# Joining the second half of a dilated-attention layer's tokens: softmax weights carried through DRAM, or built on chip and spread by TensorE

## Chip, cores and metric

One core of one Trainium2 chip. The metric is the device time of one execution in microseconds (us); the kernel before stands at 2389.81 us, the median of three runs. "Change" below means the edited kernel; a row or a page named without more belongs to the kernel before.

## What is computed

Two encoder layers over T = 1024 tokens of D = 1024 features, each a token mixer and a SwiGLU FFN with a pre-RMSNorm and a gated residual. The second layer's mixer is dilated attention in three head groups; only its join is touched:

```
for gi, (window, dil) in enumerate(((128, 1), (512, 4), (2048, 16))):
    o, lse = banded_attention(to_strided(q[:, :, gi], dil), ...)   # 8 query heads, 2 KV heads, 64 wide
    outs.append(from_strided(o, b, dil)); lses.append(from_strided(lse, b, dil))
alpha = softmax(stack(lses), axis=0)          # weight of each group, per position and head
o = einsum('nbshg,nbshgd->bshgd', alpha, stack(outs))
return o.reshape(b, s, 512) @ w_out
x = x + g1 * y;  h = rmsnorm(x, norm_ffn) * (1 + sc2) + sh2
x = x + g2 * ((silu(gate) * up) @ ffn_w_out)
```

## The kernel before

Activations lie with features on the partitions, D as eight k-tiles of 128 rows, the tokens as two halves t = 0 and 1 of HT = 512 columns. Each fp32 product of a weight and an activation is three matmuls on split operands (`acc3`, L297): high by high (L300), high by low (L301), low by high (L302). A weight tile arrives by a DMA (`load_w`, L182), is rounded by ScalarE (L179) and its low part is subtracted by GpSimd (L180).

Layer 2 (`layer_b`, L907) runs 48 units of attention. A unit's first half (`probs`, L495) is scores on TensorE (L506, L507), bias and minimum on VectorE (L509) and exponentials on ScalarE (L514). Its second half (`weigh`, L517) transposes the probabilities (L534), splits them into high and low part (ScalarE L536, VectorE L537), multiplies by the values (L528) and writes the output (ScalarE L549, VectorE L550). Between the units TensorE is fed from a list of fill work in a fixed order, with a table of due points (`fill_start`, FILL_B): projections, then the out-projection of the first token half (`out_0`; residual L370, squares L217 and L218), that half's norm (`norm_half`; sums L222, statistics on GpSimd, broadcast L260, then L272, L273, L275, L276, L278 per k-tile) and, last, 48 matmuls of the FFN's first feature block on that half (`up_early`).

Groups 1 and 2 hold their tokens in strided order, and their outputs go to DRAM (od[1], od[2]) and come back. The softmax statistics take this way: `stat_out` (L1052) transposes minimum and sum of a group and half (copy L1062, TensorE L1063, ScalarE L1070) and stores them (sd, DMAs L1068, L1072, L1075). `alphas(t)` (L1077) loads the three groups' statistics (ml_all, L1082), permutes them into token order (VectorE copies L1086 to L1088), forms the weights in small operations on 64 partitions (L1090 to L1100, exponential L1094) and stores them (ad, L1101). `combine_load` (L1121) loads two groups' outputs (al<-od, L1114, L1115) and the weights, each row repeated over 64 partitions (al<-ad, L1128). `combine` (L1131) forms, per 128 rows g of 0 to 3, o2 and o3 times their weights (L1141, L1143), o1 times its weight (L1145, on GpSimd for t = 1), two sums (L1146, L1147), and the high and low part for the out-projection (ScalarE L1148, VectorE L1149).

The first half is joined at units 33 to 37. The second half is joined after the last unit: `stat_out(0, 1)`, `alphas(1)`, `combine_load(1, 0)`, the last units' second halves, `combine_load(1, 1)`, `combine(1, 0)`, `combine(1, 1)`. Then `swiglu(0, 0)` (silu L415, product L417, split L418 and L419) and two feature blocks for the first token half, `up(1, (0,))` and `up(2, (0,))`, 48 matmuls L300 to L302 each with two weight tiles; then the second half's out-projection (96 matmuls), its norm, and the rest of the FFN for both halves. A scheduler places every instruction in its engine's queue at build time; each engine then runs its queue strictly in order.

Of the kernel before, what the change touches and what calls it, by code (L numbers as in the profile page):

```python
# [18 lines left out]
HT = 512  # L19
# [38 lines left out]
def f32(ap):  # L58
    return ap.bitcast(F)
# [15 lines left out]
class Trunk:  # L75
# [831 lines left out]
    def layer_b(self, h, x_src):  # L907
        nc, a, sb = self.nc, self.a, self.sb
# [5 lines left out]
        sd = [[dram.tile([2, 64, 64], F, name=f"sd{t}_{i}") for i in range(3)] for t in range(2)]  # L914
# [5 lines left out]
        self.norm_bank = self.bank  # L920
        kp = es.enter_context(sb("att_b"))
        self.raw = deque([(self.main, 1), (kp, 1)])
        stats = [kp.tile([P, 2, 8, 2, 4], F, name=f"stat{i}") for i in range(3)]
        dist = {}
        for gi in range(3):
            off, n = DIST[gi]
# [176 lines left out]
        def tile2(pool, tag, n):  # L1103
            return pool.tile([P, 2, HT], F, name="al", tag=tag, bufs=n)

        def out_load(t, i):

            if t == 0:
                x = self.htile([2, 2, HT], F)
                got = [x[:, 0], x[:, 1]]  # L1110
            else:
                got = [tile2(wk, *c) for c in (("q2", 2), ("pp", 3))[i:i + 1] * 2]
            g = slice(2 * i, 2 * i + 2)
            nc.sync.dma_start(got[0], od[1][:, g].rearrange("p g (r i) -> p g r i", r=4)[:, :, :, t * P:(t + 1) * P].rearrange("p g r i -> p (g r) i"))  # L1114
            nc.sync.dma_start(got[1], od[2][:, g, t])  # L1115
            if t == 0:
                y = self.htile([2, 2, HT], F)
                got += [y[:, 0], y[:, 1]]
            return got

        def combine_load(t, i):  # L1121

            got = out_load(t, i)
            rest = (("p", 3),) * 3 if t == 1 and i == 0 else (("pp", 3), ("v", 2), ("v", 2))
            got += [tile2(wk, *c) for c in rest[len(got) - 2:]]
            for gi in range(3):
                for kv in range(2):
                    nc.sync.dma_start(got[2 + gi][64 * kv:64 * kv + 64], ad[t][gi][4 * kv + 2 * i:4 * kv + 2 * i + 2].unsqueeze(0).broadcast_to([64, 2, HT]))  # L1128
            return got

        def combine(t, i, got):  # L1131

            if i == 0:
                oTs[t] = [self.htile([4, HT]) for _ in range(2)]
            oT = oTs[t]
            for j in range(2):
                g = 2 * i + j
# [49 lines left out]
        for i, (gi, kv, u) in enumerate(units):  # L1187
            self.fill_until(need.get(i, 0))
            if i % 2 == 0:
                q2 = wk.tile([P, 4, 256], R, name="q2", tag="q2", bufs=2)  # L1190
                src = qd[gi, :, kv].rearrange("g p c -> p g c")
                if gi == 2:
                    for j in range(2):
                        for t in range(2):
                            c, d = 64 * (2 * j + t), t * HT + 64 * (u + j)
                            nc.sync.dma_start(f32(q2[:, :, c:c + 64]), src[:, :, d:d + 64])
                else:
                    c = u % 2 * HT + u // 2 * P if gi else u * P
                    nc.sync.dma_start(f32(q2), src[:, :, c:c + 256])
            if i in (0, 8) or i >= 16 and i % 4 == 0:  # L1200
                bias = self.bias_tiles(wk, dist[gi], SLOPE_B[8 * gi + 4 * kv:8 * gi + 4 * kv + 4], 5)
                v = v_load(gi, kv, i // 32)
            pend.append((gi, kv, u) + self.weave(i, first(gi, kv, u, q2, bias, v), second(*pend.popleft()) if len(pend) > 1 else None))
            if i == 17:
                for t in range(2):
                    stat_out(2, t)
            elif i in (25, 41):
                stat_out(1, i // 40)
            elif i == 33:
                stat_out(0, 0)  # L1210
                alphas(0)
                got[0] = combine_load(0, 0)
            elif i in (35, 37):
                combine(0, (i - 35) // 2, got[0])
                if i == 35:
                    got[0] = combine_load(0, 1)
                else:
                    self.most = 1000
        while self.fill:
            self.fill_step()  # L1220
        stat_out(0, 1)
        alphas(1)
        got = [combine_load(1, 0)]
        while pend:
            run(second(*pend.popleft()))
        got.append(combine_load(1, 1))
        for i in range(2):
            combine(1, i, got[i])
        es.close()

        self.ffn_begin(layer, "b", 4, ORDER_B)
# [91 lines left out]
def _arrays(np, i):  # L1323

    c = np.ascontiguousarray

    def cols(w, idx):

        w = w[:, idx]
        return c(w.reshape(KT, P, -1, P).transpose(2, 1, 0, 3)).reshape(-1, P, D)  # L1330

    def per_part(v):
        return v.reshape(-1, P).T

# [4 lines left out]
    o["sel"] = np.kron(np.ones((2, 1)), np.kron(np.eye(8).reshape(8, 2, 4).transpose(0, 2, 1).reshape(8, 8), np.ones((1, 64)))).astype(np.float32)  # L1339
    o["sink"] = c(i["a_sink"])  # L1340
# [44 lines left out]
```

## Time and profile before

| | |
|---|---|
| median of three runs | 2389.81 us (2389.62 to 2392.29) |
| the profiled execution | 2388.49 us, its trace spans 2386.7 us |
| TensorE (PE) busy | 2265.4 us, 95% |
| VectorE (DVE), ScalarE (ACT), GpSimd (POOL) busy | 1229.5, 845.4, 719.9 us |
| mean granted clock | 0.973 of 2.4 GHz |
| chain that ended last | PE 75%, DVE 9%, DMA 6% |

Times in a row are microseconds from the start of the span. In a timeline a row is the start, the duration, the engine, the program line with output and inputs, how many such instructions stand in a row, and in square brackets how long the engine had been idle and what ended that. In the windows view each row is a stretch: its length, then busy time of PE, the weight loads, DVE, ACT and POOL with the number of instructions, the granted TensorE clock (1.00 is 2.4 GHz), the share of the DMA engines and GB/s.

### The profile page before, as it was taken

How to read it: one execution, taken by the hardware profiler on the slowest of the kernel's cores; microseconds unless marked ns; L12 is line 12 of the kernel's file. 1: busy time of each engine (PE TensorE's matmuls, PEld its weight loads, DVE VectorE, ACT ScalarE, POOL GpSimd, SP SyncE). 2: the span in 40 equal slices, each digit the busy share in tenths (PEclk: the TensorE clock that was granted, in tenths of full speed). 3: DMA queues.
4: the chain of work that ended last, by engine and by line, in shares of the span. 5: the costliest groups of instructions: out<-in, count | busy, mean ns of one | idle time of the engine just before them, and what ended most of it. 6: DMA issues, size and time to landing. Idle time of an engine off the chain costs nothing.

```text
span 2386.7 us, 28047 instructions
## 1 busy us (share of the span) xinstructions
PE 2265.4 (95%) x10604; PEld 1878.6 (79%) x10604; DVE 1229.5 (52%) x2103; ACT 845.4 (35%) x1654; POOL 719.9 (30%) x451
## 2 busy tenths in 40 slices
PE   8699998989999999999999999787999999999997
PEld 7588887767888888888878878576788888888886
DVE  7868876787522233333452667776633333222325
ACT  2548876231111111111243878573311111111111
POOL 2524433452222221222133344434422222222210
PEclk9899999999999999999989999898999999999999
DMA  7441134766311111111245765726321111111101
GB/s 285 151 144 36 48 99 141 243 225 198 124 53 49 49 45 44 45 53 44 93 139 151 201 173 179 212 75 212 99 70 45 53 44 53 54 53 45 53 18 71
DMA packets 131255, 248.87 MB, mean 104 GB/s; under 512 B 39328, under 2 KB 66592, under 8 KB 130096
## 3 DMA queue, kind: packets, MB, share of 16 engines
q1 hardware_dynamic: 131120, 247.08, 32.5%
q8 instruction: 83, 1.36, 0.2%
q14 instruction: 52, 0.43, 0.1%
HBM read 214.24 MB, written 30.70 MB: 103 GB/s over the span
## 4 chain that ended last, share of the span: by engine, by line
PE 75%; DVE 9%; DMA 6%; issue 2%; ACT 2%; POOL 1%; SPq 0%; DVEq 0%; ACTq 0%; POOLq 0%
PE ps_d L300 23%; PE ps_d L302 23%; PE ps_d L301 23%; DMA ada_w<-in_ada_w 3%; DVE ada_acc L152 2%; PE ps_o L528 2%; PE ps_t L534 2%; PE ps_s L507 1%; PE ps_s L506 1%; DMA ml_all<-sd 1%; DVE ht L272 1%; DVE p L509 1%; DVE h L278 1%; DVE pp L537 1%; DVE x L370 1%
## 5 line engine op out<-in xcount | busy, mean ns | idle before, releaser
L300 PE MATMUL ps_d<-h,w 128*128 128x512 f32 x1968 | 778.5, 398 | 25.2 <-ACT w L179 11.5
L301 PE MATMUL ps_d<-h,w 128*128 128x512 f32 x1968 | 777.9, 395 | 10.1 <-DVE h L278 9.3
L302 PE MATMUL ps_d<-h,w 128*128 128x512 f32 x1968 | 774.8, 394 | 2.8 <-POOL w L180 2.7
L180 POOL TENSOR_TENSOR w<-raw,w 128x1024 fp32r<-128x1024 f32 (+1 forms) x178 | 430.9, 2423 | 844.8 <-ACT w L179 816.8
L300 PEld LDWEIGHTS ps_d<-h,w 128*128 128x128 f32 x1968 | 374.4, 191 | 97.9 <-ACT w L179 13.2
L301 PEld LDWEIGHTS ps_d<-h,w 128*128 128x128 f32 x1968 | 375.7, 191 | 83.0 <-DVE h L278 11.5
L302 PEld LDWEIGHTS ps_d<-h,w 128*128 128x128 f32 x1968 | 374.5, 190 | 83.8 <-POOL w L180 4.9
L417 DVE TENSOR_TENSOR u<-silu,ps_d 128x512 f32<-128x512 f32 x88 | 60.4, 686 | 601.5 <-PE ps_d L302 584.5
L370 DVE SCALAR_TENSOR_TENSOR x<-ps_d,mod,x 128x512 f32<-128x512 f32 x368 | 270.3, 747 | 144.9 <-PE ps_d L302 142.3
L179 ACT ACTIVATE w<-raw 128x1024 fp32r<-128x1024 f32 (+1 forms) x178 | 185.5, 1046 | 377.2 <-PE ps_d L302 299.3
L300 PE MATMUL ps_d<-act,wo 128*128 128x512 f32 x704 | 275.8, 392 | 8.1 <-DVE u L417 4.3
L301 PE MATMUL ps_d<-act,wo 128*128 128x512 f32 x704 | 274.7, 390 | 0.0
L302 PE MATMUL ps_d<-act,wo 128*128 128x512 f32 x704 | 274.6, 390 | 0.0
L180 POOL TENSOR_TENSOR wo<-raw,wo 128x1024 fp32r<-128x1024 f32 x44 | 105.7, 2402 | 433.5 <-ACT wo L179 426.1
L179 ACT ACTIVATE wo<-raw 128x1024 fp32r<-128x1024 f32 x44 | 46.7, 1060 | 384.7 <-PE ps_d L302 340.2
L300 PEld LDWEIGHTS ps_d<-act,wo 128*128 128x128 f32 x704 | 132.5, 188 | 38.3 <-DVE x L370 5.6
L302 PEld LDWEIGHTS ps_d<-act,wo 128*128 128x128 f32 x704 | 132.6, 188 | 27.8
L301 PEld LDWEIGHTS ps_d<-act,wo 128*128 128x128 f32 x704 | 132.5, 188 | 27.2
L419 DVE TENSOR_TENSOR act<-u,act 128x512 fp32r<-128x512 f32 x88 | 123.4, 1403 | 48.8 <-ACT act L418 48.8
L152 DVE SCALAR_TENSOR_TENSOR ada_acc<-ada_w,cond,ada_acc 128x1024 f32<-128x1024 f32 x70 | 122.2, 1746 | 47.5 <-DMA ada_w<-in_ada_w 46.5
L418 ACT ACTIVATE act<-u 128x512 fp32r<-128x512 f32 x88 | 55.0, 625 | 217.7 <-DVE u L417 217.4
L537 DVE TENSOR_TENSOR pp<-ps_t,pp 128x512 fp32r<-128x512 f32 x168 | 115.3, 688 | 15.6 <-ACT pp L536 13.7
(182 smaller groups left out, 2543.7 us busy)
## 6 DMA issues: line engine op xcount, KB each, us to landing
raw<-in_ffn_w_in SPq DMA_DIRECT2D x102, 512.0 KB
ada_w<-in_ada_w SPq DMA_DIRECT2D x80, 512.0 KB
raw<-in_ffn_w_out SPq DMA_DIRECT2D x44, 512.0 KB
raw<-in_b_w_q SPq DMA_DIRECT2D x24, 512.0 KB
qd<-qo SPq DMA_DIRECT2D x48, 256.0 KB
h<-in_ada_w SPq DMA_DIRECT2D x8, 1024.0 KB
raw<-in_a_w_out SPq DMA_DIRECT2D x16, 512.0 KB
q<-qd SPq DMA_DIRECT2D x16, 512.0 KB
```

Of the source, the lines that this page charges most:

```text
L152: nc.vector.scalar_tensor_tensor(acc, w, s, acc, op0=ALU.mult, op1=ALU.add)
L179: self.nc.scalar.activation(w[:, 0], raw, AF.Copy)
L180: self.nc.gpsimd.tensor_tensor(w[:, 1], raw, f32(w[:, 0]), op=ALU.subtract)
L300: mm(ps, lhsT=w[0], rhs=x[0], start=first, stop=False)
L301: mm(ps, lhsT=w[0], rhs=x[1], start=False, stop=False)
L302: mm(ps, lhsT=w[1], rhs=x[0], start=False, stop=last)
L370: self.nc.vector.scalar_tensor_tensor(x, ps, self.mod[:, layer, c * 8 + d:c * 8 + d + 1], x, op0=ALU.mult, op1=ALU.add)
L417: nc.vector.tensor_tensor(u, s, up, op=ALU.mult)
L418: nc.scalar.activation(act[:, 0, halves(t)], u, AF.Copy)
L419: nc.vector.tensor_tensor(act[:, 1, halves(t)], u, f32(act[:, 0, halves(t)]), op=ALU.subtract)
L528: nc.tensor.matmul(po, lhsT=v, rhs=pp[:, s], start=(i == 0 and s == 0), stop=(i == len(chunks) - 1 and s == 1))
L537: nc.vector.tensor_tensor(pp[n, 1], tp[n], f32(pp[n, 0]), op=ALU.subtract)
```

## The change

A 48 by 1536 matrix of zeros and ones (`sel`) is loaded at the start of layer 2 in three pieces and copied by ScalarE. For t = 1, `stat_out(0, 1)`, `alphas`, `combine_load` and `combine` go. In their place: `relay(1)` after unit 44 brings the statistics of groups 1 and 2 back from DRAM in token order and transposes them to tokens on the partitions; `weights(1)` (group 0's statistics never left the chip) forms the weights there, splits them, and transposes them to 48 rows; `join` spreads a row over 64 partitions with one matmul by `sel` per group, three per g, into PSUM, and multiplies from there. Its sums are in PSUM too, and o1's product is on VectorE. The first half keeps the DRAM path. Lines below are those of the changed kernel (`relay` L1148 to L1160, `weights` L1162 to L1197, `join` L1199 to L1221).

```diff
+        sel = kp.tile([48, 12 * P], R, name="sel")
+        for i in range(3):
+            raw = kp.tile([48, HT], F, name="sel_f", tag="qo", bufs=3)
+            nc.sync.dma_start(raw, a["sel_b"][:, i * HT:(i + 1) * HT])
+            nc.scalar.activation(sel[:, i * HT:(i + 1) * HT], raw, AF.Copy)          # L927
+        st12 = kp.tile([P, 4, 4, 8], F, name="st12")
...
+        def relay(t):
+            rl = wk.tile([P, HT], F, name="rl", tag="t2", bufs=self.t2)[0:32].rearrange("p (x j) -> p x j", x=4)
+            rp = wk.tile([P, HT], F, name="rp", tag="t2", bufs=self.t2)[0:32].rearrange("p (x j) -> p x j", x=4)
+            for gi in (2, 1):
+                x = slice(2 * gi - 2, 2 * gi)
+                nc.sync.dma_start(rl[:, x], sd[t][gi]...)                            # L1154
+                nc.vector.tensor_copy(rp[:, x]..., rl[:, x]...)                      # L1156
+            for x in range(4):
+                nc.tensor.transpose(tp[:, 32 * x:32 * x + 32], rp[:, x], ...)        # L1159
+            nc.scalar.activation(st12..., tp..., AF.Copy)                            # L1160
+        def weights(t):
...
+            v(top, m[:, 0], m[:, 1], op=ALU.min)                                     # L1176
...
+            v(fv[:, :, :, 1], wv, f32(fv[:, :, :, 0]), op=ALU.subtract)              # L1191
...
+            for u in range(4):
+                nc.tensor.transpose(tp[0:48, u * P:(u + 1) * P], f32(fl[:, u]), ...) # L1194
+            nc.scalar.activation(rows, tp[0:48], AF.Copy)                            # L1196
+        def join(t, g, got, rows):
+            for gi in range(3):
+                ps = psp.tile([P, HT], F, name="ps_al", tag="os"[gi > 0], bufs=2)
+                nc.tensor.matmul(ps, lhsT=sel[:, c:c + P], rhs=rows, ...)            # L1209
+                al.append(ps)
+            s = al[0]
+            v(w2..., o2..., al[1]..., op=ALU.mult)                                   # L1214
+            v(w3..., o3..., al[2]..., op=ALU.mult)                                   # L1215
+            v(s, o1[t][:, g], s, op=ALU.mult)                                        # L1217
+            v(s, s, w2, op=ALU.add)                                                  # L1218
+            v(s, s, w3, op=ALU.add)                                                  # L1219
+            nc.scalar.activation(oT[0][:, g], s, AF.Copy)                            # L1220
+            v(oT[1][:, g], s, f32(oT[0][:, g]), op=ALU.subtract)                     # L1221
...
+            elif i == 44:
+                relay(1)
...
-        stat_out(0, 1)
-        alphas(1)
-        got = [combine_load(1, 0)]
+        rows = weights(1)
+        got = ...
+        for i in range(2):
+            load_12(1, i, got[i])
         while pend:
             run(second(*pend.popleft()))
-        got.append(combine_load(1, 1))
-        for i in range(2):
-            combine(1, i, got[i])
+        for g in range(4):
+            join(1, g, got[g // 2], rows)
```

The scheduler lays the queues out anew. TensorE's queue before, from the last matmul of `up_early` to the first of `up(1)`; ps_t and ps_o are transposes and outputs of units:

```order
L302 MATMUL ps_d<-h,w 128x512
L534 MATMUL ps_t<-cst,p 128x128 x4
L528 MATMUL ps_o<-pp,v 128x512 x2
L534 MATMUL ps_t<-cst,p 128x128 x4
L528 MATMUL ps_o<-pp,v 128x512 x2
L534 MATMUL ps_t<-cst,p 128x128 x4
L528 MATMUL ps_o<-pp,v 128x512 x4
L300 MATMUL ps_d<-h,w 128x512
```

TensorE's queue in the change, the last 20 instructions ahead of the first matmul of `up(1)`, which is the last row; ps_al are the spread weights:

```order
L1209 MATMUL ps_al<-al_r,sel 128x512 x2
L528 MATMUL ps_o<-pp,v 128x512 x2
L534 MATMUL ps_t<-cst,p 128x128 x4
L528 MATMUL ps_o<-pp,v 128x512
L1209 MATMUL ps_al<-al_r,sel 128x512
L528 MATMUL ps_o<-pp,v 128x512
L534 MATMUL ps_t<-cst,p 128x128 x4
L1209 MATMUL ps_al<-al_r,sel 128x512
L528 MATMUL ps_o<-pp,v 128x512 x3
L1209 MATMUL ps_al<-al_r,sel 128x512
L528 MATMUL ps_o<-pp,v 128x512
L1209 MATMUL ps_al<-al_r,sel 128x512 x7
L300 MATMUL ps_d<-h,w 128x512
```

Before, two units' second halves stand between `up_early` and `up(1)`, and no part of the join is in this queue. Now the second halves of the last five units (nine of their ten sets of transposes L534, 20 matmuls L528), the last six pairs of scores and all twelve spreading matmuls stand there, after `up_early`'s last matmul.

VectorE's queue in the change, from the last unit's last output to the low part of g = 1:

```order
L1217 TENSOR_TENSOR ps_al<-o_1_9711,ps_al 128x512 x2
L1218 TENSOR_TENSOR ps_al<-ps_al,w_13248 128x512
L1219 TENSOR_TENSOR ps_al<-ps_al,w_13249 128x512
L1214 TENSOR_TENSOR w_13263<-ol,ps_al 128x4x128
L1215 TENSOR_TENSOR w_13264<-ol,ps_al 128x16x32
L1218 TENSOR_TENSOR ps_al<-ps_al,w_13263 128x512
L1221 TENSOR_TENSOR h<-ps_al,h 128x512
L1219 TENSOR_TENSOR ps_al<-ps_al,w_13264 128x512
L1214 TENSOR_TENSOR w_13278<-ol,ps_al 128x4x128
L1215 TENSOR_TENSOR w_13279<-ol,ps_al 128x16x32
L1217 TENSOR_TENSOR ps_al<-o_1_9711,ps_al 128x512
L1221 TENSOR_TENSOR h<-ps_al,h 128x512
```

The last L1209 writes the bank that L1221 of g = 1, the last row, reads: it is issued only when these 13 operations are over, and `up(1)` stands behind it.

ScalarE's queue in the change, from the last unit's output copy (os) to `up(2)`'s weights:

```order
L549 ACTIVATE os<-ps_o 64x512
L1220 ACTIVATE h<-ps_al 128x512 x2
L415 ACT_TABLE_LOAD
L415 ACTIVATE silu<-ps_d 128x512
L1220 ACTIVATE h<-ps_al 128x512
L179 ACTIVATE w<-raw 128x1024
L418 ACTIVATE act<-u 128x512
L1220 ACTIVATE h<-ps_al 128x512
L415 ACTIVATE silu<-ps_d 128x512
L179 ACTIVATE w<-raw 128x1024 x2
```

The first L415 writes memory that lay under `sel`, so it waits for the last L1209. The first L179 is the second weight of `up(1)`: it stood ahead of the join's copies before, and now stands behind three of the four. The two L179 at the end are `up(2)`'s.

## Rows read from the trace of the kernel before

**Rows 1.** The page's first and fifth part: busy times, and the weight split's groups
```profile
PE 2265.4 (95%) x10604; PEld 1878.6 (79%) x10604; DVE 1229.5 (52%) x2103; ACT 845.4 (35%) x1654; POOL 719.9 (30%) x451
...
L180 POOL TENSOR_TENSOR w<-raw,w 128x1024 fp32r<-128x1024 f32 (+1 forms) x178 | 430.9, 2423 | 844.8 <-ACT w L179 816.8
...
L179 ACT ACTIVATE w<-raw 128x1024 fp32r<-128x1024 f32 (+1 forms) x178 | 185.5, 1046 | 377.2 <-PE ps_d L302 299.3
```
**Rows 2.** Windows around the second half's join, columns as explained above
```profile
1602.00:1610.00 8.00, 8.00 (x34) 6.56 (x33) 2.71 (x9) 3.75 (x8) 2.57 (x2) 0.91 0.04 8
1610.00:1617.00 7.00, 4.69 (x23) 2.98 (x22) 4.66 (x10) 5.05 (x8) 5.13 (x2) 1.00 0.54 129
1617.00:1628.00 11.00, 10.89 (x48) 8.66 (x47) 3.43 (x4) 0.60 (x1) 1.29 (x1) 1.00 1.04 274
1628.00:1637.00 9.00, 0.14 (x1) 0.14 (x1) 7.88 (x12) 3.00 (x5) 2.26 (x2) 0.65 0.60 152
1637.00:1645.00 8.00, 5.77 (x14) 3.87 (x15) 7.97 (x5) 2.01 (x3) 6.97 (x3) 0.54 0.23 68
```
**Rows 3.** Timeline of TensorE, 1565 to 1653 us
```profile
1565.52 0.50 PE L300 MATMUL ps_d<-h,w 128*128 128x512 f32 x1 [0.81 <-DVE h L370]
...
1576.27 0.71 PE L528 MATMUL ps_o<-pp,v 128*128 128x512 f32 x2
...
1610.13 0.60 PE L534 MATMUL ps_t<-cst,p 128*128 128x128 f32 x4
...
1616.83 0.40 PE L300 MATMUL ps_d<-h,w 128*128 128x512 f32 x1
...
1627.51 0.39 PE L302 MATMUL ps_d<-h,w 128*128 128x512 f32 x1
1636.86 0.80 PE L300 MATMUL ps_d<-h,w 128*128 128x512 f32 x1 [8.96 <-ACT w L179]
...
1641.25 0.80 PE L302 MATMUL ps_d<-h,w 128*128 128x512 f32 x1 [2.23 <-POOL w L180]
...
1643.12 0.63 PE L300 MATMUL ps_d<-h,w 128*128 128x512 f32 x1
1643.55 0.63 PE L301 MATMUL ps_d<-h,w 128*128 128x512 f32 x1
...
1652.81 0.39 PE L300 MATMUL ps_d<-h,w 128*128 128x512 f32 x1
```
**Rows 4.** Timeline of VectorE, 1560 to 1629 us
```profile
1560.89 0.21 DVE L1086 COPY wt<-ml_all 64x64 f32<-64x64 f32 x1 [2.58 <-DMA ml_all<-sd]
...
1587.65 2.06 DVE L272 SCALAR_TENSOR_TENSOR ht<-h,gain,ps_d 128x512 f32<-128x512 f32 x3
...
1607.41 0.22 DVE L1091 TENSOR_TENSOR top<-top,ml_all 64x64 f32<-64x64 f32 x1 [3.33 <-DMA ml_all<-sd]
...
1617.66 0.68 DVE L550 TENSOR_TENSOR o<-ps_o,os 64x512 f32<-64x512 f32 x1 [1.22 <-ACT os L549]
1625.22 1.08 DVE L1141 TENSOR_TENSOR w<-al 128x512 f32<-128x512 f32 x1 [6.88 <-DMA al<-ad]
...
1628.12 0.69 DVE L1147 TENSOR_TENSOR s<-s,w 128x512 f32<-128x512 f32 x1
```
**Rows 5.** Timeline of ScalarE: start of layer 2, and the join
```profile
1208.60 0.59 ACT L954 ACTIVATE kh<-ps_d 64x512 fp32r<-64x512 f32 x1 [3.77 <-PE ps_d L302]
...
1608.57 1.28 ACT L415 ACT_TABLE_LOAD   x1
...
1634.61 0.63 ACT L1148 ACTIVATE h<-s 128x512 fp32r<-128x512 f32 x1 [5.12 <-DVE s L1147]
```
**Rows 6.** Timeline of GpSimd: the last low part of the norm
```profile
1604.05 1.29 POOL L276 TENSOR_TENSOR h<-ht,h 128x512 fp32r<-128x512 f32 x1 [0.58 <-ACT ht L275]
```
**Rows 7.** Timeline of the DMA queue (start and length of the issue)
```profile
1605.33 0.58 SPq L1082 DMA_DIRECT2D ml_all<-sd  x1
1610.34 1.79 SPq L1101 DMA_DIRECT2D ad<-wt  x3
```

More of the change, by code (lines that the diff above doesn't have):

```diff
@@ L1104, in tile2, with load_12 @@
             return pool.tile([P, 2, HT], F, name="al", tag=tag, bufs=n)
[L1106 to L1112, printed above, removed]
+        def load_12(t, i, got):
             g = slice(2 * i, 2 * i + 2)
@@ L1115, in out_load @@
             nc.sync.dma_start(got[1], od[2][:, g, t])
[L1116 to L1119, printed above, removed]
         def combine_load(t, i):
-            got = out_load(t, i)
-            rest = (("p", 3),) * 3 if t == 1 and i == 0 else (("pp", 3), ("v", 2), ("v", 2))
-            got += [tile2(wk, *c) for c in rest[len(got) - 2:]]
+            x, y = (self.htile([2, 2, HT], F) for _ in range(2))
+            got = [x[:, 0], x[:, 1], y[:, 0], y[:, 1], tile2(wk, "v", 2)]
+            load_12(t, i, got)
             for gi in range(3):
@@ L1149, in combine @@
                 e[5].tensor_tensor(oT[1][:, g], s, f32(oT[0][:, g]), op=ALU.subtract)
+        def relay(t):
[3 more added lines that the diff above has]
+                x = slice(2 * gi - 2, 2 * gi)
+                nc.sync.dma_start(rl[:, x], sd[t][gi].rearrange("s (a c) j -> a s (c j)", c=2))
+                i = 16 // (1, 1, 4)[gi]
+                nc.vector.tensor_copy(rp[:, x].rearrange("p s (c i r) -> p (s c) i r", c=2, i=i), rl[:, x].rearrange("p s (c r i) -> p (s c) i r", c=2, i=i))
+            tp = psp.tile([P, HT], F, name="ps_t", tag="t", bufs=2)[:, 0:P]
+            for x in range(4):
+                nc.tensor.transpose(tp[:, 32 * x:32 * x + 32], rp[:, x], self.ident[0:32, 0:32])
+            nc.scalar.activation(st12.rearrange("p x u h -> p x h u"), tp.rearrange("p (x h u) -> p x h u", x=4, h=8), AF.Copy)
@@ new lines, in weights, with by_unit @@
+        def weights(t):
+            us = slice(4 * t, 4 * t + 4)
+            def by_unit(ap):
+                return ap.rearrange("p (u k g) -> p u k g", u=4, k=2)
+            we = wk.tile([P, 192], F, name="al_w", tag="wt", bufs=1)
+            m0, l0 = (stats[0][:, :, us, s].rearrange("p k u g -> p u k g") for s in range(2))
+            m, l = (st12[:, s:4:2].rearrange("p x u h -> p x (u h)") for s in range(2))
+            w, e = (x.rearrange("p (x j) -> p x j", x=3) for x in (we[:, 0:96], we[:, 96:192]))
+            top = wk.tile([P, P], F, name="al_t", tag="top", bufs=1)[:, 0:32]
+            v = nc.vector.tensor_tensor
+            v(top, m[:, 0], m[:, 1], op=ALU.min)
+            v(by_unit(top), by_unit(top), m0, op=ALU.min)
+            v(by_unit(w[:, 0]), by_unit(top), m0, op=ALU.subtract)
+            v(w[:, 1:3], top.unsqueeze(1).broadcast_to([P, 2, 32]), m, op=ALU.subtract)
+            nc.scalar.activation(w, w, AF.Exp)
+            v(by_unit(e[:, 0]), by_unit(w[:, 0]), l0, op=ALU.mult)
+            v(e[:, 1:3], w[:, 1:3], l, op=ALU.mult)
+            v(top, e[:, 0], e[:, 1], op=ALU.add)
+            v(top, top, e[:, 2], op=ALU.add)
+            nc.vector.reciprocal(top, top)
+            v(w, w, top.unsqueeze(1).broadcast_to([P, 3, 32]), op=ALU.mult)
+            fl = wk.tile([P, 384], R, name="al_f", tag="ml_all", bufs=1)[:, 0:192].rearrange("p (u x) -> p u x", u=4)
+            fv = fl.rearrange("p u (x s h) -> p x u s h", x=3, s=2)
+            wv = w.rearrange("p x (u h) -> p x u h", u=4)
+            nc.scalar.activation(fv[:, :, :, 0], wv, AF.Copy)
+            v(fv[:, :, :, 1], wv, f32(fv[:, :, :, 0]), op=ALU.subtract)
+            tp = psp.tile([P, HT], F, name="ps_t", tag="t", bufs=2)
+            for u in range(4):
+                nc.tensor.transpose(tp[0:48, u * P:(u + 1) * P], f32(fl[:, u]), self.ident)
+            rows = wk.tile([P, HT], R, name="al_r", tag="t2", bufs=self.t2)[0:48]
+            nc.scalar.activation(rows, tp[0:48], AF.Copy)
+            return rows
@@ new lines, in join @@
+        def join(t, g, got, rows):
+            if g == 0:
+                oTs[t] = [self.htile([4, HT]) for _ in range(2)]
+            oT = oTs[t]
+            o2, o3 = (x[:, g % 2] for x in got)
+            al = []
+            for gi in range(3):
+                ps = psp.tile([P, HT], F, name="ps_al", tag="os"[gi > 0], bufs=2)
+                c = (4 * gi + g) * P
+                nc.tensor.matmul(ps, lhsT=sel[:, c:c + P], rhs=rows, start=True, stop=True)
+                al.append(ps)
+            s = al[0]
+            w2, w3 = (wk.tile([P, HT], F, name=n, tag="t2", bufs=self.t2) for n in ("w2", "w3"))
+            v = nc.vector.tensor_tensor
+            v(w2.rearrange("p (i r) -> p r i", r=4), o2.rearrange("p (r i) -> p r i", r=4), al[1].rearrange("p (i r) -> p r i", r=4), op=ALU.mult)
+            v(w3.rearrange("p (i j r) -> p j r i", j=8, r=2), o3.rearrange("p (j r i) -> p j r i", r=2, i=32),
+              al[2].rearrange("p (i j r) -> p j r i", j=8, r=2), op=ALU.mult)
+            v(s, o1[t][:, g], s, op=ALU.mult)
[3 more added lines that the diff above has]
+            v(oT[1][:, g], s, f32(oT[0][:, g]), op=ALU.subtract)
@@ L1220, in layer_b @@
             self.fill_step()
-        stat_out(0, 1)
-        alphas(1)
-        got = [combine_load(1, 0)]
+        rows = weights(1)
+        got = [[wk.tile([P, 2, HT], F, name="ol", tag=tag, bufs=n) for tag, n in x] for x in ((("q2", 2), ("q2", 2)), (("v", 2), ("p", 3)))]
+        for i in range(2):
+            load_12(1, i, got[i])
         while pend:
             run(second(*pend.popleft()))
-        got.append(combine_load(1, 1))
-        for i in range(2):
-            combine(1, i, got[i])
+        for g in range(4):
+            join(1, g, got[g // 2], rows)
         es.close()
@@ L1339, in _arrays @@
     o["sel"] = np.kron(np.ones((2, 1)), np.kron(np.eye(8).reshape(8, 2, 4).transpose(0, 2, 1).reshape(8, 8), np.ones((1, 64)))).astype(np.float32)
+    o["sel_b"] = np.kron(np.eye(3), np.kron(np.ones((2, 1)), np.kron(np.eye(8).reshape(8, 2, 4).transpose(0, 2, 1).reshape(8, 8), np.ones((1, 64))))).astype(np.float32)
     o["sink"] = c(i["a_sink"])
```

## The prediction

> **What bounds the kernel now.** I read the page first, then the windows around the join, then the timeline of each engine in those windows. TensorE is busy for 2265.4 us of a span of 2386.7 [rows 1], and both its work before the join and its work after it are the same in the change. So the question is how long TensorE stands still between the last common point before the join and the next one behind it, and which engine it waits for there. The windows [rows 2] show where: from 1610 to 1617 it is busy for 4.69 of 7 us (second halves of units with nothing beside them), from 1617 to 1628 for 10.89 of 11 (`up(1)` at full rate), from 1628 to 1637 for 0.14 of 9, and from 1637 to 1645 for 5.77 of 8 at a granted clock of 0.54, so mostly at the lower level of 1.2 GHz. In TensorE's timeline [rows 3] these are: `up_early` ends and bare units begin at 1610.13; `up(1)` runs from 1616.83 to 1627.51; a wait of 8.96 us for `up(2)`'s weight, one of 2.23 us for its low part, and the out-projection of the second half starts at 1652.81. The first of these waits is the join's: ScalarE rounds that weight only after the join's copies, one of which waited 5.12 us for VectorE [rows 5], and VectorE itself had stood 6.88 us for the weights' way through DRAM [rows 4]. But `up(1)` hid 10.7 us of the join, because it needed nothing from it.
>
> **The change part by part.** I walk the change's queues in order, with durations of this trace, and compare at the start of the second half's out-projection.
>
> (a) `alphas(1)` and its loads go. VectorE's wait of 2.58 us at 1560.89 [rows 4] is for the first statistics of `alphas(1)` and goes too. VectorE then evacuates TensorE's banks later, but TensorE lost only 0.81 us by it [rows 3], so it is worth −0.8 us at the common point of the two queues, the pair of L528 at 1576.27 [rows 3].
>
> (b) The norm of the first half follows. Its three first scalings L272 stand at 1587.65 [rows 4] and come, by (a), at about 1586.9. In the change they, and the rest of the norm's VectorE operations, are placed ahead of the units' work; the last low part on GpSimd, at 1604.05 + 1.29 [rows 6], comes at about 1599.8.
>
> (c) The relay. Its two loads take up memory that GpSimd's L276 reads, so they go out near 1597.2 and 1597.8. No row shows a load of this form; the nearest is the load of the statistics, issued at 1605.33 [rows 7] and awaited until 1607.41 [rows 4], 2.1 us. With that, L1156 is over by about 1600.7, and its transposes hold TensorE up little. TensorE, fed by an earlier norm, ends `up_early` at 1603 to 1604.5, and I take 1603.9: some 6 us ahead of 1610.13.
>
> (d) What was gained is then laid out bare. Two units' second halves alone took 1616.83 − 1610.13 = 6.7 us [rows 3], 3.35 each. The change's queue has five there: 16.8 us. The weights' small operations add about 2.2 us to VectorE's queue (twelve of 0.2 us, by the 0.22 of L1091 [rows 4], some of it hidden). g = 0's two products add 2 × 1.08 [rows 4] = 2.2 us. That gives 1603.9 + 16.8 + 2.2 + 2.2 = 1625.1. Behind the last unit come the 13 operations that the queue in the section on the change shows: nine at 0.69 and four at 1.08 [rows 4], 10.5 us, which gives 1635.6. They wait on each other across TensorE, ScalarE and VectorE (a product needs its L1209, L1221 needs L1220), for which I add 1.4 us: the last L1209 and the start of `up(1)` at **1637**, against 1616.83.
> No row has these products with the weights in PSUM or the sums written to it. Between 0.69 (L550, which reads PSUM) and 1.08 (L1141, strided like the products) [rows 4] I take 1.08 for the products, whose strides are the same, and 0.69 for the sums. With 0.69 for all, 1.6 us less; with 1.08 for all, 3.5 us more.
>
> (e) `up(1)`'s first weight is ready, so five matmuls go at once. Its second is not: L179 now stands behind three of the join's copies, the silu (which waits for the last L1209) and so behind g = 2's sums. 2 × 0.69 + 0.63 [rows 4, 5] + 1.05 + 2.40 (the split's two groups [rows 1]) = 5.5 us: 1642.5.
>
> (f) 43 matmuls at (1627.51 − 1616.83) / 47 = 0.227 us [rows 3] are 9.8 us. At the lower clock one takes 1643.55 − 1643.12 = 0.43 us [rows 3]; I charge eleven of them, as the trace has after its 8.96 us wait, 2.2 us: 1654.5.
>
> (g) `up(2)`'s weights stand behind the silu of `up(1)`: 0.6 + 1.05 + 2.40 us less 1.4 us in which the last matmuls still run, 2.6 us: 1657.1. Its remaining 44 matmuls take 10.0 us: the out-projection starts at **1667.1**.
>
> Against 1652.81 that is **+14.3 us**. What costs nothing: the three copies of `sel` fall into ScalarE's 3.77 us of idleness at the start of layer 2 [rows 5]; 18 more matmuls lie in TensorE's waits of (d); the table load of 1.28 us [rows 5] waits beside TensorE's join. The second join's twelve weight loads and three weight stores on SP's queue go, and nobody waits for what is behind them. GpSimd loses four products and had time. Behind the out-projection the two programs are the same, so nothing is given back.
>
> 2388.49 + 14.3 = 2402.8 us for an execution like the profiled one; that execution is 1.3 us below the median, so the forecast for a median is **2404 us**.
>
> **Rivals.**
>
> *Faster (F): the join no longer waits for DRAM.* From the weights' store at 1610.34 [rows 7] to the first product at 1625.22 [rows 4] 14.9 us pass, of which VectorE stood for 6.88. If the join were done by the time `up(2)` wants its weights, TensorE's 8.96 and 2.23 us and the 2.2 us of low clock would go: 13.4 us, 2376 us. For it speaks that these waits are real and that the change removes two of the hops that caused them. It decides if the twelve L1209 could be passed before TensorE runs out of other work; against it stands TensorE's queue, where all of them and five units precede `up(1)`, so that the 10.7 us of cover are gone. The Trainium skill, "DMA: Bandwidth & Descriptors", section "Latency and other measured facts", puts a fixed cost of about 2 us on each DMA, most of it the receipt round trip to memory; by it alone two hops fewer are an estimated 4 us less, 2386 us. The trace agrees on the single hop (2.1 us [rows 4, 7]).
>
> *No change (S): the bare stretch is only as long as VectorE is busy.* VectorE's own work from 1603.9 on is 27.9 us (10.5 + 2.2 + 2.2, ten L537 and five L550 at 0.69, and 2.6 for the last scores). With no idleness `up(1)` would start at 1631.8, 5.2 us earlier than in (d), and if TensorE's clock stayed up and `up(2)`'s weights came in time, 4.8 us more go: +4.3, 2394 us. Against it: in the bare 7 us before, VectorE was busy for 4.66 only [rows 2].
>
> *A greater loss (G): TensorE's clock stays down.* Between 1628 and 1645 it fell to 0.65 and 0.54 after the long wait, though not from 1610 to 1617, when the waits were short [rows 2]. If the bare stretch leaves it down until `up(1)` is over, 43 × (0.43 − 0.227) = 8.7 us take the place of 2.2: +20.8, 2411 us. The Trainium skill, "TensorE: Matmul & The Clock Gate", section "HAM oscillation — how this bites in real kernels", describes a TensorE that waits between short bursts of matmuls, is throttled again in each wait and starts each burst cold; by it the time would be that 2411. The trace here bears out the fall after a long wait and the return within some 7 us of work, which is why G is not the forecast.
>
> **How the numbers follow.** About 0.2% (4.8 us) is what a measurement of this kernel can tell from no change. Forecast 0.75, F 0.09, S 0.08, G 0.08. The low end is S's 2394; the high end takes G's 2411 with 3 us for dearer PSUM operands, 2414; F lies outside. Faster 0.09; within 0.2% 0.08 (S); slower 0.83.
>
> **What would show it.** In the changed kernel's profile: no wait for ml_all near 1560; `up_early` ended near 1604; then TensorE less than half busy until `up(1)` starts near 1637; a second wait there for GpSimd's L180 until about 1642.5, behind L1220 and the silu on ScalarE; the out-projection near 1667. If `up(1)` starts before 1625, or its second weight is ready by then, the forecast is wrong and F or S holds; if its matmuls stand 0.43 us apart throughout, G does. An out-projection that starts before 1653 would overturn the whole argument.

## The result and the profile after

The change takes 2402.94 us (median of five runs, 2401.65 to 2403.55) against 2389.62 us for the kernel before: ratio 1.0051, 95% interval [1.0041, 1.0062], 13.3 us slower by the medians. (A ratio is estimated from the single runs; it is not the quotient of the medians, which would be 1.0056 here.) A second series gave 2408.59 against 2392.74, ratio 1.0062 [1.0042, 1.0083]. 2404 us within 2394 to 2414 had been forecast.

Single executions of one program lie up to 15 us apart (2382.00 to 2396.56 us in one series below), and part of that is there before layer 2 begins, where TensorE's queue is the same in both programs. So I compare two stretches between marks that every trace has: TensorE's sums of a norm (L222, eight matmuls of one column). **A** runs from the last sums of layer 1 to those of the first token half in layer 2, **J** (the join's) from there to those of the second half. TensorE's timeline of the kernel before:

```profile
1203.00 0.95 PE L222 MATMUL ps_d<-ones,ssq 128*128 128x1 f32 x8
...
1580.79 1.05 PE L222 MATMUL ps_d<-ones,ssq 128*128 128x1 f32 x8 [0.32 <-DVE ssq L218]
...
1681.37 0.95 PE L222 MATMUL ps_d<-ones,ssq 128*128 128x1 f32 x8
```

And of the change, with the rows that answer to [rows 3]:

```profile
1202.78 0.95 PE L222 MATMUL ps_d<-ones,ssq 128*128 128x1 f32 x8
...
1575.64 1.05 PE L222 MATMUL ps_d<-ones,ssq 128*128 128x1 f32 x8 [0.87 <-DVE ssq L218]
...
1599.15 0.43 PE L1159 MATMUL ps_t<-cst,rp 32*128 32x32 f32 x4
...
1600.69 0.39 PE L302 MATMUL ps_d<-h,w 128*128 128x512 f32 x1
1600.92 0.60 PE L534 MATMUL ps_t<-cst,p 128*128 128x128 f32 x4
...
1613.45 1.02 PE L1194 MATMUL ps_t<-cst,al_f 128*48 128x128 f32 x4 [2.40 <-DVE al_f L1191]
...
1623.39 0.79 PE L1209 MATMUL ps_al<-al_r,sel 48*128 48x512 f32 x1 [1.40 <-DVE o L550]
1627.40 1.66 PE L1209 MATMUL ps_al<-al_r,sel 48*128 48x512 f32 x2 [3.22 <-DVE w L1214]
...
1633.08 0.79 PE L1209 MATMUL ps_al<-al_r,sel 48*128 48x512 f32 x1 [0.39 <-DVE h L1221]
1633.80 0.79 PE L300 MATMUL ps_d<-h,w 128*128 128x512 f32 x1
...
1638.43 0.79 PE L302 MATMUL ps_d<-h,w 128*128 128x512 f32 x1 [0.87 <-POOL w L180]
...
1651.89 0.50 PE L300 MATMUL ps_d<-h,w 128*128 128x512 f32 x1 [0.95 <-ACT w L179]
...
1694.43 0.95 PE L222 MATMUL ps_d<-ones,ssq 128*128 128x1 f32 x8
```

A went from 377.8 to 372.9 us, J from 100.6 to 118.8: 4.9 less and 18.2 more, together 13.3. Of the 4.9 only 1.7 lie behind the wait that the change removes; the rest lies ahead of it, at a higher granted clock, and differs from execution to execution (shown with the run no_early_wait). Inside J, `up_early` ends at 1600.92, then 32.9 us pass until `up(1)` starts at 1633.80, where 6.7 had passed before [rows 3]. The out-projection starts at 1665.87, 13.06 us later than before, and the trace's span is 2399.8 us against 2386.7, 13.1 us more: nothing is given back behind it.

Windows of the change, columns as in [rows 2]:

```profile
1601.00:1613.00 12.00, 8.46 (x45) 5.74 (x43) 10.25 (x34) 9.33 (x27) 2.65 (x2) 0.86 0.67 194
1613.00:1623.00 10.00, 8.51 (x33) 5.25 (x33) 5.76 (x9) 4.18 (x8) 0.00 (x0) 0.83 0.22 86
1623.00:1634.00 11.00, 5.67 (x8) 2.19 (x9) 10.71 (x16) 2.57 (x4) 0.00 (x0) 0.51 0.00 0
1634.00:1644.00 10.00, 8.20 (x19) 5.49 (x20) 6.58 (x10) 3.16 (x5) 2.37 (x1) 0.51 0.60 214
1644.00:1651.00 7.00, 6.93 (x31) 5.42 (x29) 0.00 (x0) 0.71 (x2) 0.00 (x0) 1.00 0.82 293
1651.00:1658.00 7.00, 5.14 (x14) 3.54 (x15) 2.18 (x2) 2.30 (x3) 5.14 (x2) 0.76 0.20 77
```

From 1623 to 1634 VectorE is busy for 10.71 of 11 us, and TensorE issues eight matmuls in that time: this is the join, laid bare. A busy time for TensorE at a clock of 0.51 says little; the count of matmuls does. VectorE's timeline of the change:

```profile
1594.70 1.24 DVE L1156 COPY rp<-rl 32x256 f32<-32x256 f32 x2 [2.26 <-DMA rl<-sd]
1600.05 0.19 DVE L1176 TENSOR_TENSOR al_t<-st 128x32 f32<-128x32 f32 x1 [4.11 <-ACT st L1160]
...
1616.05 0.69 DVE L537 TENSOR_TENSOR pp<-ps_t,pp 128x512 fp32r<-128x512 f32 x1 [2.75 <-ACT pp L536]
1616.92 1.10 DVE L1214 TENSOR_TENSOR w<-ol,ps_al 128x512 f32<-128x512 f32 x1 [0.18 <-PE ps_al L1209]
...
1622.65 0.68 DVE L550 TENSOR_TENSOR o<-ps_o,os 64x512 f32<-64x512 f32 x1 [1.21 <-ACT os L549]
1623.37 0.69 DVE L1217 TENSOR_TENSOR ps_al<-o,ps_al 128x512 f32<-128x512 f32 x1
...
1632.33 0.69 DVE L1221 TENSOR_TENSOR h<-ps_al,h 128x512 fp32r<-128x512 f32 x1
```

The join's VectorE operations run all but back to back (one gap, of 0.15 us) from 1623.37 to 1633.02, and the last L1209 follows the last of them at 1633.08. VectorE had stood still twice earlier: 2.26 us for the relay's load and 4.11 us for its transposes, which were ready to run at 1595.94 but stood behind `up_early`'s matmuls in TensorE's queue. ScalarE's timeline of the change shows the weight behind the join:

```profile
1633.91 0.60 ACT L415 ACTIVATE silu<-ps_d 128x512 f32<-128x512 f32 x1 [1.98 <-PE ps_al L1209]
1634.40 0.59 ACT L1220 ACTIVATE h<-ps_al 128x512 fp32r<-128x512 f32 x1
1634.89 1.05 ACT L179 ACTIVATE w<-raw 128x1024 fp32r<-128x1024 f32 x1
```

### The profile page after: what moved, and what is told of

Its sections match the earlier page's. It is cut to its first block, busy times and chain, and to the rows that moved or that the text cites. A ratio compares the mean times of both kernels' runs of the same rounds, so it can differ in the third digit from the quotient of the medians.

```text
span 2399.8 us, 28061 instructions
## 1 busy us (share of the span) xinstructions
PE 2276.2 (95%) x10622; PEld 1881.7 (78%) x10622; DVE 1225.2 (51%) x2100; ACT 848.1 (35%) x1658; POOL 709.6 (30%) x447
## 5 line engine op out<-in xcount | busy, mean ns | idle before, releaser
L370 DVE SCALAR_TENSOR_TENSOR x<-ps_d,mod,x 128x512 f32<-128x512 f32 x368 | 270.2, 747 | 145.0 <-PE ps_d L302 144.9
L179 ACT ACTIVATE w<-raw 128x1024 fp32r<-128x1024 f32 (+1 forms) x178 | 185.7, 1046 | 371.6 <-PE ps_d L302 298.1
L179 ACT ACTIVATE wo<-raw 128x1024 fp32r<-128x1024 f32 x44 | 46.7, 1060 | 382.1 <-PE ps_d L302 340.3
```

What stands on the lines that cost most here:

```text
L179: self.nc.scalar.activation(w[:, 0], raw, AF.Copy)
L370: self.nc.vector.scalar_tensor_tensor(x, ps, self.mod[:, layer, c * 8 + d:c * 8 + d + 1], x, op0=ALU.mult, op1=ALU.add)
```

## The experiments

Theory Q: the loss is the order that the queues were given. The relay borrows the norm's buffers, so it cannot load before the norm is nearly done, and the norm and `up_early` come to stand ahead of five units; and the spreading matmuls wait for VectorE through PSUM banks, with `up(1)` behind them. Rival V: VectorE's work behind the last unit sets the end, whatever stands ahead. Rival W: forming the weights on chip costs by itself.

All traces, with A and J in us (differences of rows like those above), and the time as a ratio to the kernel before on the same chip. A and J are those of one traced execution, which can lie some us off its kernel's median (five_early's took 2393.62 us, its median is 2396.09): they show where the time goes, and the ratio shows how much.

| kernel | A | J | median us | ratio [95%] |
|---|---|---|---|---|
| before; again | 377.8; 378.5 | 100.6; 102.1 | 2389.62 | 1 |
| change; again | 372.9; 373.3 | 118.8; 118.5 | 2402.94; 2408.59 | 1.0051 [1.0041, 1.0062]; 1.0062 [1.0042, 1.0083] |
| relay_own | 371.5 | 109.0 | 2394.39 | 1.0023 [1.0013, 1.0033] |
| spread_copy | 375.1 | 113.8 | 2397.71 | 1.0028 [1.0019, 1.0037] |
| relay_copy | 376.3 | 103.2 | 2390.87 | 1.0004 [0.9994, 1.0013] |
| weights_dram | 374.4 | 110.3 | 2396.54 | 1.0027 [1.0017, 1.0037] |
| weights_dram_own | 372.7 | 109.1 | 2392.17 | 1.0006 [0.9996, 1.0016] |
| early_spread | 375.1 | 108.1 | 2395.32 | 1.0021 [1.0010, 1.0031] |
| o1_vector | 376.9 | 100.5 | 2392.55 | 0.9994 [0.9985, 1.0003] |
| five_early | 375.1 | 104.2 | 2396.09 | 1.0018 [1.0009, 1.0028] |
| five_early_vector | 375.1 | 100.4 | 2392.70 | 0.9998 [0.9984, 1.0011] |
| no_early_wait | 373.3 | 100.2 | 2390.71 | 0.9991 [0.9981, 1.0000] |

**Two more traces.** The kernel before and the change, as they are.

> The kernel before, a second trace. From the norm sums of the first half to those of the second half it took 100.6 us (1580.8 to 1681.4); the five other traces took 374.0 us on average for the stretch ahead of it, this kernel 377.8. If that lead is the lost wait of 2.58 us and its followers, this trace shows 377 to 378 again and 100 to 101 for the join's stretch; if it is chance, the stretch ahead is near 374.

> The changed kernel, a second trace on the same chip as the run before it. From norm sums to norm sums 118 to 119 us again (118.8 in the first trace), the stretch ahead 372 to 376 us, and a ratio to the kernel before of 1.005 to 1.006.

A and J repeat to 0.7 and 1.5 us for the kernel before (378.5, 102.1) and to 0.4 and 0.3 for the change (373.3, 118.5). The loss in J is the change's, not chance. Of the lead in A that can't be said: the eleven traces of kernels with the weights on chip lie between 371.5 and 376.9 us, 374.4 on average, against 378.2 for the two without, and two of the eleven, alike up to the join, took 345.15 us (relay_own) and 350.56 us (o1_vector) for the same 1690 matmuls up to VectorE's first L370 of the first half's residual, at mean granted clocks of 0.96 and 0.94.

**The relay in memory of its own.**

```diff
-            rl = wk.tile([P, HT], F, name="rl", tag="t2", bufs=self.t2)...
-            rp = wk.tile([P, HT], F, name="rp", tag="t2", bufs=self.t2)...
+            rl = kp.tile([P, HT], F, name="rl", tag="qo", bufs=3)...
+            rp = kp.tile([P, HT], F, name="rp", tag="qo", bufs=3)...
```

> The changed kernel, with the relay's two tiles in memory of their own instead of the norm's buffers. Theory Q (the loss is the order that the queues were given: the relay shares buffers with the norm, so the norm and up_early stand ahead of five units, which then run bare; and the spreading matmuls wait for VectorE through PSUM banks): the units lie beside the norm and up_early again, up_early ends near 1606 us, up(1) starts near 1622 instead of 1633.8, 2392 us (2389 to 2396). Rival V (VectorE's own work behind the last unit sets the end, whatever the order ahead): 2403 us (2400 to 2405).

Its transposes L1159 come at 1565.04, ahead of the norm sums, and the units lie beside the norm and `up_early` again. TensorE's timeline, from `up_early`'s last matmul to `up(1)`:

```profile
1605.16 0.39 PE L302 MATMUL ps_d<-h,w 128*128 128x512 f32 x1
1605.39 0.38 PE L1194 MATMUL ps_t<-cst,al_f 128*48 128x128 f32 x2
...
1615.27 0.50 PE L1209 MATMUL ps_al<-al_r,sel 48*128 48x512 f32 x1 [1.40 <-DVE o L550]
1619.03 1.66 PE L1209 MATMUL ps_al<-al_r,sel 48*128 48x512 f32 x2 [3.26 <-DVE w L1214]
...
1625.41 0.79 PE L300 MATMUL ps_d<-h,w 128*128 128x512 f32 x1
```

J falls by 9.8 us, the time to 2394.39, inside the range that Q gave, though `up(1)` starts at 1625.41 and not near 1622. The bare stretch is 20.0 us (1605.39 to 1625.41) instead of 32.9; `up_early` itself ends later after the norm sums (30.1 us against 25.3), since units lie in it. V, with its 2403, falls as the whole cause.

**The spread weights copied out of PSUM.** The join of the kernel before on tiles that ScalarE fills.

```diff
+                nc.tensor.matmul(ps, lhsT=sel[:, c:c + P], rhs=rows, start=True, stop=True)
+                nc.scalar.activation(got[2 + gi][:, g % 2], ps, AF.Copy)
...
+        for i in range(2):
+            combine(1, i, got[i])
```

> The changed kernel, with each spread weight tile copied from PSUM to memory by ScalarE at once, and the join's products and sums as in the kernel before (o1's on GpSimd). Theory Q: the spreading matmuls no longer wait for VectorE; the last stands some 5 us behind the last unit's output instead of 10.4, up(1) starts near 1628, 2396 us (2393 to 2399). Rival V: VectorE has the same products and sums to make, so 2403 us (2400 to 2406).

> Both edits of the two runs before. Theory Q: the two causes add up, up(1) starts near 1616 as in the kernel before the change and the join lies beside it without a wait for DRAM, 2386 us (2381 to 2391). Rival V: within 3 us of 2403.

The edit does more than one thing: it frees the banks after a copy, and it takes the sums out of PSUM and o1's product off VectorE. Alone it takes 5.0 us off J, with the relay's memory 15.6 (the two alone: 9.8 + 5.0 = 14.8). So these two causes make up 15.6 of the 18.2 us that J had lost, and they add within the 1.5 us to which J repeats. The times agree: 1.0028, and 1.0004 for both, no longer to be told from the kernel before. `up(1)` starts at 1624.65, though, and not near 1616 as Q had it. TensorE's timeline of relay_copy shows what is left:

```profile
1623.44 1.28 PE L1204 MATMUL ps_al<-al_r,sel 48*128 48x512 f32 x2 [0.26 <-ACT al L1205]
1624.65 0.79 PE L300 MATMUL ps_d<-h,w 128*128 128x512 f32 x1
...
1640.39 0.50 PE L300 MATMUL ps_d<-h,w 128*128 128x512 f32 x1 [2.25 <-ACT w L179]
...
1644.07 0.80 PE L302 MATMUL ps_d<-h,w 128*128 128x512 f32 x1 [2.94 <-POOL w L180]
```

The spreading matmuls follow one another at ScalarE's pace, `up(1)` starts behind them, and `up(2)`'s weights are late as before [rows 3], by 2.25 and 2.94 us in place of 8.96 and 2.23.

**Weights on chip, spread through DRAM.** No spreading matmul: the rows are stored to `ad`, loaded repeated, and joined as before; then the same with the relay's own memory.

```diff
+            for gi in range(3):
+                nc.sync.dma_start(ad[t][gi], rows[8 * gi:8 * gi + 8])
```

> The changed kernel's relay and weights on chip, but the weights stored to DRAM and spread by DMAs into the tiles of the kernel before, joined as there: one part of the change alone, with no spreading matmul and no sum in PSUM. Theory Q: five units stay bare, but up(1) starts right behind the last of them, near 1622 us, and hides the join: 2391 us (2387 to 2396). Rival W (forming the weights on chip is what costs: the relay's loads, the small operations, the transposes): 2403 us (2400 to 2407).

> The weights formed on chip and spread by DMAs through DRAM, now with the relay's tiles in memory of their own. Theory Q: the bare units go as they did in the run with the relay alone (9.8 us less between the two norm sums), so 2387 us (2383 to 2391) and near 100 us between the norm sums. Rival W (forming the weights on chip costs by itself): it stays at 2395 or above.

The first lies just above Q's range (2396.54 against 2396), and below W's, which began at 2400. The second gained less than forecast: 2392.17 us lies between Q's range (to 2391) and W's (from 2395), and its J is 109.1 us where Q had about 100. TensorE's timeline of the second:

```profile
1616.57 0.66 PE L534 MATMUL ps_t<-cst,p 128*128 128x128 f32 x4 [1.94 <-ACT al_r L1193]
...
1621.06 0.50 PE L528 MATMUL ps_o<-pp,v 128*128 128x512 f32 x1 [2.13 <-DVE pp L537]
...
1645.16 0.79 PE L300 MATMUL ps_d<-h,w 128*128 128x512 f32 x1 [8.90 <-ACT w L179]
```

With the spreading in DMAs, `up(2)`'s weight waits 8.90 us for the join again, as before the change (8.96 [rows 3]): that wait was for the way through DRAM, as rival F had it, and on-chip spreading does remove it. The other two waits, 1.94 and 2.13 us, lie among the last units, where the weights' rows and two roundings of weights stood ahead of the units' copies on ScalarE; to that extent W holds. This trace is the longest of its kernel's runs (2397.32 us), so its J is an upper value.

**Where o1's product and the copies go.** Three edits on relay_copy, and one that went its own way.

```diff
-COMB = "vvvpvp", "vvpvvv"
+COMB = "vvvpvp", "vvvvvv"
```

> The run with relay and copies, o1's product moved from GpSimd to VectorE. If up(2)'s second weight came late there because ScalarE's rounding of it stood behind the last copy of the join, which waited for GpSimd's product (1640.06 us) and a VectorE sum that took 2.81 us beside GpSimd's work: 2 to 3 us less, 2388 us. Rival: VectorE gets four products more (2.8 us) and the join ends as late, 2391 to 2393 us.

J falls from 103.2 to 100.5, `up(2)`'s two waits to 1.13 and 2.32 us: the reading holds in the trace. In time it isn't shown: the median of 2392.55 lies in the rival's range, on a chip where the kernel before took 2392.48 (2389.99 in relay_copy's series), and the ratio goes from 1.0004 to 0.9994 with intervals that overlap. But J does not rise with o1's product back on VectorE, so taking that product off VectorE is not what spread_copy gained by; the freed banks and the sums outside PSUM were not tested apart.

```diff
+        got[0] += [None, o1[0][:, 0:2], o1[0][:, 2:4]]
+        for g in range(2):
+            for gi in (1, 2):
+                spread(g, gi, got[0], rows, "s")
         while pend:
             run(second(*pend.popleft()))
```

> The run with relay and copies, with the spread weights of groups 1 and 2 for g = 0 and 1 put into the space of the first half's o1, which is dead by then: five instead of two spreading matmuls lie among the last units. Theory Q: fewer are left bare behind the last unit, up(1) starts 2 to 3 us earlier after the last unit, 2388 us. Rival: the copies delay the last units on ScalarE by as much, 2391 us.

> Both edits of the two runs before. If both hold, 2386 us (2382 to 2389), faster than the kernel before by some 4 us, at the edge of what can be told; if neither, 2391 us or above.

The matmuls did move among the units, but J went from 103.2 to 104.2, and with o1 on VectorE it stayed at 100.4: nothing is gained, as the rival had it. In time five_early is above both forecasts (2396.09 us, ratio 1.0018), and five_early_vector, at 2392.70, where it was put if neither edit helped. In five_early's trace one of the last units' matmuls waits 0.56 us for ScalarE, and the last spreading matmuls wait 0.26, 0.74 and 0.75 us for copies.

> The version that the runs point to: relay in memory of its own; groups 1 and 2's spread weights copied to the space of dead key tiles, so that eight of the twelve spreading matmuls can lie among the last units; group 0's weights read from PSUM by VectorE into a sum outside PSUM, so that each bank is free after one product; nothing of the join on GpSimd; the matrix of zeros and ones allocated last. Theory Q: the last spreading matmul comes 1 to 2 us behind the last unit, up(1) starts 4 us earlier than with relay and copies, up(2)'s weight waits for no sum on GpSimd: 2384 us (2379 to 2389). Rival V: VectorE's 19 us of products and sums set the end as in that run, 2391 us.

This missed both forecasts, 2384 and 2391: 2395.32 us. TensorE's timeline has two waits that relay_copy's has not:

```profile
1626.80 0.80 PE L300 MATMUL ps_d<-h,w 128*128 128x512 f32 x1 [4.64 <-DVE s L1218]
...
1638.96 0.79 PE L300 MATMUL ps_d<-h,w 128*128 128x512 f32 x1 [4.94 <-ACT w L179]
```

Group 0's weights stay in PSUM until VectorE's product L1218, and `up(1)` needs that bank. The weight behind the second wait was not rounded late by ScalarE; it was loaded late:

```profile
1637.85 1.06 ACT L179 ACTIVATE w<-raw 128x1024 fp32r<-128x1024 f32 x1 [1.04 <-DMA raw<-in_ffn_w_in]
```

The DMA queue issued that load at 1634.06, just after the last product that reads the reused key tiles had ended (1632.88 + 1.10). That the FFN's load buffer lies over those tiles fits this, but I did not test it.

**The first term by itself.** On the kernel before, only the early statistics work leaves VectorE's queue.

```diff
-                nc.vector.tensor_copy(wt[:, 1]..., ml[:, s, 1]...)
+                (nc.gpsimd if t else nc.vector).tensor_copy(wt[:, 1]..., ml[:, s, 1]...)
...
-            nc.vector.tensor_tensor(top[:, 0], m[:, 1], m[:, 2], op=ALU.min)
-            nc.vector.tensor_tensor(top[:, 0], top[:, 0], m[:, 0], op=ALU.min)
+            nc.vector.tensor_tensor(top[:, 0], m[:, 1 - t], m[:, 2 - t], op=ALU.min)
+            nc.vector.tensor_tensor(top[:, 0], top[:, 0], m[:, 2 * t], op=ALU.min)
```

> The kernel before, with the second half's early statistics work taken out of VectorE's queue alone: the copies that permute groups 1 and 2 are on GpSimd, and the first minimum takes group 0, which comes late. TensorE's order is the same but for one pair. It tests the first term of the prediction, -0.8 us for the wait of 2.58 us at 1560.89. If that wait is worth what TensorE lost at once, the stretch from the start of layer 2 to the first half's norm sums stays at 377 to 378 us; if the whole wait reaches the norm (VectorE is what those stretches wait for), it is 374 to 376 us and the time 2 to 4 us below the kernel before.

```profile
1206.46 0.95 PE L222 MATMUL ps_d<-ones,ssq 128*128 128x1 f32 x8
...
1579.75 1.05 PE L222 MATMUL ps_d<-ones,ssq 128*128 128x1 f32 x8
```

A is 373.3 us, 4.9 less than the two traces of the kernel before have on average (378.2), 0.7 below the expected range, and like the change's own 372.9 and 373.3. But most of that does not come from the wait. VectorE's last operation ahead of it, an L370 that all three kernels have, splits A. First that row and the window from the mark to it in the kernel before, then in the change, then in this run; TensorE does 1700 matmuls up to there each time, in the same order but for one:

```profile
1557.56 0.74 DVE L370 SCALAR_TENSOR_TENSOR h<-ps_d,mod,h 128x512 f32<-128x512 f32 x1
...
1203.00:1557.56 354.56, 328.89 (x1700) 277.11 (x1699) 212.25 (x599) 231.66 (x595) 139.13 (x113) 0.94 0.60 175
```

```profile
1554.09 0.74 DVE L370 SCALAR_TENSOR_TENSOR h<-ps_d,mod,h 128x512 f32<-128x512 f32 x1
...
1202.78:1554.09 351.31, 324.95 (x1700) 273.82 (x1699) 211.29 (x599) 233.40 (x598) 138.77 (x113) 0.96 0.62 178
```

```profile
1558.20 0.74 DVE L370 SCALAR_TENSOR_TENSOR h<-ps_d,mod,h 128x512 f32<-128x512 f32 x1
...
1206.46:1558.20 351.74, 324.07 (x1700) 273.54 (x1699) 211.94 (x599) 231.87 (x595) 138.49 (x114) 0.96 0.61 177
```

Ahead of the wait the kernel before took 354.56 us at a mean granted clock of 0.94, the other two 351.31 and 351.74 at 0.96. Behind it, from the L370 to the norm sums, it took 23.23 us (23.49 in its second trace), the change 21.55 (21.48) and this run 21.55: the wait is worth 1.7 to 2.0 us. VectorE itself gained more: from the end of that L370 to its next L218 5.7 us passed in the kernel before, with the wait and the copies behind it, and 0.7 in this run, but most of these 5.0 us were lost again to waits for ScalarE and TensorE before the norm sums. J keeps its 100.2. The time fits: 2390.71 against 2392.74, ratio 0.9991 with an interval that ends at 1.0000, the lowest of all versions, and not to be told from no change.

## Why the prediction was right

The total was right (+14.3 us forecast; +13.3 and +15.9 by the medians of the two series), and so was the mechanism that the sum rests on: TensorE's queue, walked in order. But single terms were off, some one way and some the other. And that the two traces differ by 13.1 us, and not by the 16.5 that the change made in them, is luck: the other 3.2 us come from ahead of the wait.

- (a) −0.8 us: measured −1.7, in the change (21.55 us for 23.23) and in the run with nothing else edited. "TensorE lost only 0.81 us by it" took the price from what the bound engine lost at once; VectorE's gain of 5.0 us was the other bound, and neither was the price. The other 3.2 us by which A was shorter in the first pair of traces lie ahead of the wait, at the clock of 0.96 against 0.94, and no term stands for them. Why the clock differed there stays open.
- (b), (c) The norm's operations did run ahead of the units; from the norm sums to `up_early`'s end 25.3 us passed, where 23.9 had been forecast (1603.9 less 1580.0). The relay's load took 1.8 us (issued at 1592.94, used at 1594.70), where 2.1 was taken. The Trainium skill, "DMA: Bandwidth & Descriptors", section "Latency and other measured facts", has about 2 us for a DMA's fixed cost; this trace agrees within 0.3 us.
- (d) 33.1 us from `up_early` to `up(1)`: measured 32.9. Single parts were off and cancelled: VectorE's 13 last operations took 9.65 us where 10.5 and 1.4 for waits were set, and from `up_early`'s end to the last unit's output it was 22.4 us where 21.2 were set, with a wait of TensorE for the weights (2.40 us) where the sum had 2.2 us of VectorE's operations. The PSUM prices fell where they were put: 1.02 to 1.10 us for the strided products, 0.67 to 0.74 for the other operations.
- (e) 5.5 us: 4.6, since L1218 and the first 0.14 us of L1219 had run when `up(1)` started (1632.93 and 1633.66 in VectorE's timeline).
- (f) 12.0 us: 12.4 (1638.43 to 1650.8). Twelve matmuls were slow, not eleven.
- (g) 12.6 us: 15.1 (1650.8 to 1665.87). Waits of 0.95, 0.21 and 0.76 us, and then seven more matmuls at about 0.43: the clock fell a second time (0.51 from 1654.3 to 1657.5), which was not in the sum.

From the norm sums to the out-projection that is +15.1 us forecast and +18.2 measured in the first trace. With (a) it is +14.3 forecast and +16.5 measured, counted from the L370 ahead of the wait; the 3.2 us ahead of that took the difference of the two traces back to 13.1.

Rival F stated the right gain at the wrong place: the waits of 8.96 and 2.23 us did go (1.92 us are left in (g)), but the join came to stand ahead of `up(1)`, and 26.2 us more of bare stretch were paid for them. weights_dram_own shows F's wait coming back with the DRAM hops. Rival S fell: from 1601 to 1634 VectorE was busy for 26.7 of 33 us, near the 27.9 that S had counted, but it also waited, 2.75 us of it at 1616.05 for copies behind the weights' transposes. Rival G fell in its strong form: the clock was at 0.51 from 1623 to 1644, its lower level of 1.2 GHz, and was 1.00 again for the 31 matmuls from 1644 on. The Trainium skill, "TensorE: Matmul & The Clock Gate", section "HAM oscillation — how this bites in real kernels", describes cold bursts between waits; the trace agrees that the join's single matmuls ran at the lower level, and that steady work brought the higher one back.

What stays open: why J of relay_copy with o1 on VectorE, at 100.5, is no better than the kernel before, though no DRAM wait is left. The rows show spreading matmuls bare at ScalarE's pace and the weight split of `up(2)` still late; no run took these away without adding a wait elsewhere.

## What to carry to other kernels

When a wait is replaced by on-chip work, read where the new instructions stand in the queue of the engine that is the bound: here the last seven of twelve small matmuls took 10.4 us (1623.39 to 1633.80), because each bank came free only after VectorE's products and sums on it, and the work that could have covered them stood behind them. A new step that borrows another step's buffers is tied to that step's end, and its queue order drags everything behind it; giving the relay two idle tiles took back 9.8 us. And price a removed wait between two marks that both kernels have, the first of them right ahead of it: here neither the 0.81 us that the bound engine lost at that moment, nor the 5.0 us that VectorE gained, nor the 4.9 us by which a longer stretch was shorter was its worth, which was 1.7.

## What the runs showed of the hardware

TensorE's clock fell after short waits too. Between 1650.8 and 1654.3 the change's TensorE stood for 0.95, 0.21 and 0.76 us, and the next seven matmuls were about 0.43 us apart; the granted clock was 0.51 from 1654.3 to 1657.5. Before the change it had kept its full clock (1.00) from 1610 to 1617 [rows 2], with longer waits, one of them this row of its timeline:

```profile
1612.90 0.50 PE L528 MATMUL ps_o<-pp,v 128*128 128x512 f32 x1 [1.27 <-ACT pp L536]
```

So the length of a wait alone did not tell. The mean clock of a long stretch also differed between executions: for the 1700 matmuls ahead of the wait it was 0.94 in both traces of the kernel before (354.56 and 355.02 us), and 0.96 and 0.95 in the two of the change (351.31 and 351.79). And the kernels' executions part before any edit: the last norm sums of layer 1, up to which TensorE's queue is the same in the kernel before and the change, came between 1201.7 and 1210.2 us in the fourteen traces. These 8.5 us are more than most effects studied here, and the reason for comparing stretches between marks.
